# Adding the second parts of an expert's rows in PSUM with a shifted identity, and taking silu and product ahead of the transposes

## The chip, the core and the metric

The kernel runs on one core of a Trainium2 chip. What counts is device time in microseconds (us), as the median of several runs. The engines carry the names that the profile gives them: PE does matrix multiplies and PEld loads their stationary operands, DVE is the vector engine, ACT the scalar engine, POOL the general one, and SP issues most of the transfers from device memory (HBM). PE writes to PSUM only, and ACT and DVE read from there. Each engine takes its own instructions in the order in which they were written.

## What is computed

Two decoder layers on 256 positions of width 1024. Each has a mixer (gMLP and gated linear attention) and a feed-forward part; the second layer's is a mixture of eight experts, of which each position uses two. The change touches this mixture alone:

```
def swiglu(x, w_gate, w_up, w_down):
    return (jax.nn.silu(x @ w_gate) * (x @ w_up)) @ w_down

    top_val, top_idx = lax.top_k(logits, TOP_K)
    top_w = jax.nn.softmax(top_val, axis=-1)
    ...
    for e in range(N_EXPERTS):
        out = out + gates[:, e:e + 1] * swiglu(t, e_gate[e], e_up[e], e_down[e])
```

An expert's hidden width is 3584, so its three weight matrices hold 44 MB in float32, and all eight have to be read.

## The kernel before

**Precision in two parts.** Weights and activations are float32. Each is split into a high part `h`, which ACT writes as a rounded copy (`split`, L271), and a remainder `l`, which DVE gets by subtraction (L272). A product of two such numbers takes the passes high x high, high x low and low x high on PE.

**Rows of an expert.** The kernel counts at run time how many positions chose an expert, and `cases` (L964) picks one of two branches by it. With more than 64 positions ("many", a wide expert) the 128 rows of the stationary operand are 128 positions. With 64 or fewer ("few") rows 0 to 63 hold the high parts of the positions and rows 64 to 127 their remainders. One pass against the weights' high part then gives high x high in the upper half of the result and low x high in the lower half, and the pass that a wide expert needs for its remainders (`rest` in `last_passes`, L1028) falls away. The price is that the two halves have to be added later.

**Groups.** An expert's 3584 hidden columns are taken in four groups, of 512, 1024, 1024 and 1024 columns (the last expert in the opposite order). A group of 1024 fills two PSUM banks of 512 columns, so an expert has seven banks. For each group the kernel issues the gate product (`product`, tiles `eg`), the copy out of PSUM (`gated`), the up product (tiles `eu`), and `finish`. Then comes the down product of the group before (`down`, L1123 on), since the results of this one are not ready yet.

**Where the halves are added before.** In the few branch, `gated` copies the whole gate bank to `sg` in SBUF (L1075, on ACT), and `finish` copies the up bank to `up` (L1085, ACT). `finish` is a task that runs beside the next products: it lets 13 ticks pass (a tick is one step of the product loops, usually two matmuls), then does the first bank's `transposed`, and 4 ticks later the second's. The transposes are multiplies with `fold`, a 128 x 64 matrix of two identities on top of each other. Such a multiply transposes 128 columns and adds the two halves at once. Both `sg` and `up` go through it:

```
for i, t in enumerate((sg, up)):
    for j in range(4):
        nc.tensor.matmul(tp[:, j, i * HALF:i * HALF + HALF], hidden_columns(t, j), fold,
                         start=True, stop=True)
nc.scalar.activation(hid, tp[:, :, 0:HALF], AF.Silu)
nc.vector.tensor_tensor(hid, tp[:, :, HALF:P], hid, op=ALU.mult)
nc.vector.tensor_copy(ch[:, :, 0:HALF], hid)
nc.vector.tensor_tensor(ch[:, :, HALF:P], hid, ch[:, :, 0:HALF].bitcast(F32), op=ALU.subtract)
```

So silu (L1110, ACT), the product with the up half (L1111, DVE) and the two parts of the result (L1112 and L1113, DVE) come after the transposes, on 64 x 128 columns per 128 rows. The result `ch` is the stationary operand of this group's down product. A wide expert takes silu in `gated`, the product in `finish` (`times`, L714), and ordinary transposes (L1117).

**What sets the order of the weights.** SP loads the weights in units of 1 MB into 18 slots, in a fixed sequence, as soon as the program finds a slot empty (`Stream`, L169). A unit is converted, which is one L271 on ACT and one L272 on DVE into two further slots, up to 12 ticks ahead of its use; the first unit of most gate products is used unconverted instead (L1050). `tick` runs the waiting tasks and then issues the conversions that are due. The conversions thus stand on ACT and DVE between the instructions of `gated`, `finish` and `transposed`, in one sequence.

Of the kernel before, what the change touches and what calls it, by code (L numbers as in the profile page):

```python
# [39 lines left out]
def trunk(ctx: ExitStack, tc: tile.TileContext, x, w_in, gm_ws, gm_bs, gm_ln_g, gm_ln_b, gla_wa2, gla_ba,  # L40
# [17 lines left out]
    def s2(name, dt=F32, shape=(P, 512)):  # L58
        return act.tile(list(shape), dt, tag="s2", name=name, bufs=6)
# [748 lines left out]
    def moe_constants():  # L808
        iota = const.tile([P, P], F32, name="iota")
        nc.gpsimd.iota(iota, pattern=[[1, P]], base=0, channel_multiplier=0, allow_small_or_imprecise_dtypes=True)  # L810
        pri = const.tile([P, NE], F32, name="pri")
        nc.gpsimd.iota(pri, pattern=[[-1, NE]], base=NE, channel_multiplier=0, allow_small_or_imprecise_dtypes=True)
        one = const.tile([P, 1], F32, name="one")
        nc.gpsimd.memset(one, 1.0)
        ecst = const.tile([P, 2], F32, name="ecst")
        nc.gpsimd.memset(ecst, 2.718281828459045)
        pair = const.tile([2 * NE, NE], F32, name="pair")
        nc.vector.tensor_tensor(pair, ident[0:2 * NE, 0:NE], ident[0:2 * NE, NE:2 * NE], op=ALU.add)
        powers = const.tile([P, NE], F32, name="powers")
        for e in range(NE):  # L820
            nc.gpsimd.memset(powers[:, e:e + 1], float(2 ** e))

        fold = const.tile([P, HALF], F32, name="fold")
        nc.vector.tensor_tensor(fold, ident[:, 0:HALF], ident[:, HALF:P], op=ALU.add)
        return iota, pri, one.to_broadcast([P, P]), ecst, pair, fold, powers

    def moe(xT, ready, consts):
# [123 lines left out]
        class Expert:  # L951
# [36 lines left out]
            def parts(self, h, l, src):  # L988

                def few():  # L990
                    nc.scalar.activation(h[:, :, 0:HALF], src[:, :, 0:HALF], AF.Copy)
                    nc.vector.tensor_tensor(h[:, :, HALF:P], src[:, :, 0:HALF], h[:, :, 0:HALF].bitcast(F32),
                                            op=ALU.subtract)
                self.cases(few, lambda: split(h, l, src))

            def pick(self, p, src, columns=block_columns):

# [27 lines left out]
                            nc.scalar.activation(self.xw, p, AF.Copy)  # L1025
                        yield 2

            def last_passes(self, rest, last):  # L1028

                def run(ms):  # L1030
# [4 lines left out]
            def product(self, units, n, nm):  # L1035

                xh, xl = self.x
                nb = n // 512
                p = [psw(f"{nm}{b}") for b in range(nb)]
                kk = 2048 // n  # L1040
                held, rest, last = [], [], []
                for u, ((wh, wl), free, drop) in enumerate(units):
                    held.append(free)
                    for j in range(kk):
                        k = kk * u + j
                        for b in range(nb):
                            s = slice(b * 512, b * 512 + 512)
                            tick()
                            if wl is None:
                                nc.tensor.matmul(p[b], self.xw[:, k, :], wh[:, j, s], start=k == 0, stop=False,  # L1050
                                                 skip_group_check=True)
                                continue
                            nc.tensor.matmul(p[b], xh[:, k, :], wh[:, j, s], start=k == 0, stop=False,  # L1053
                                             skip_group_check=True)
                            rest.append((p[b], xl[:, k, :], wh[:, j, s], False))
                            second = p[b], xh[:, k, :], wl[:, j, s], k == KT - 1
                            if k == KT - 1 or (u % 2, j, b) == (1, kk - 1, nb - 1):
                                last.append(second)
                            else:
                                nc.tensor.matmul(*second[0:3], start=False, stop=False, skip_group_check=True)  # L1060
                    if u % 2 == 0:
                        drop()
                    if u % 2 and (nb > 1 or u == 1):
                        self.last_passes(rest, last)
                        for free in held:
                            free()
                        held, rest, last = [], [], []
                return p

            def gated(self, pg, nm):  # L1070
                t = [s2(f"sg{nm}{b}") for b in range(len(pg))]

                def all(f):
                    for o, i in zip(t, pg):
                        nc.scalar.activation(o, i, f)  # L1075
                self.cases(lambda: all(AF.Copy), lambda: all(AF.Silu))
                return t

            def finish(self, g, sg, pu, lag=13):
                nm = f"e{self.nm}{g}"  # L1080
                up = [s2(f"up{nm}{b}") for b in range(len(pu))]

                def copies():
                    for o, i in zip(up, pu):
                        nc.scalar.activation(o, i, AF.Copy)  # L1085

                def products():
                    for o, i in zip(sg, pu):
                        times(o, i)
                self.cases(copies, products)  # L1090
                self.hT[g] = []
                for b in range(len(pu)):
                    yield 4 if b else lag
                    self.hT[g].append(self.transposed(f"{nm}{b}", sg[b], up[b]))
                W.cap = len(W.plan)

            def transposed(self, nm, sg, up):
# [4 lines left out]
                hid = room[-1].tile([P, 4, HALF], F32, tag="hid", name=f"hid{nm}", bufs=2)  # L1102

                def few():

                    for i, t in enumerate((sg, up)):
                        for j in range(4):
                            nc.tensor.matmul(tp[:, j, i * HALF:i * HALF + HALF], hidden_columns(t, j), fold,  # L1108
                                             start=True, stop=True)
                    nc.scalar.activation(hid, tp[:, :, 0:HALF], AF.Silu)  # L1110
                    nc.vector.tensor_tensor(hid, tp[:, :, HALF:P], hid, op=ALU.mult)  # L1111
                    nc.vector.tensor_copy(ch[:, :, 0:HALF], hid)  # L1112
                    nc.vector.tensor_tensor(ch[:, :, HALF:P], hid, ch[:, :, 0:HALF].bitcast(F32), op=ALU.subtract)  # L1113

                def many():
                    for j in range(4):
                        nc.tensor.transpose(tp[:, j, :], hidden_columns(sg, j), ident)  # L1117
                    split(ch, cl, tp)
                self.cases(few, many)
                return ch, cl  # L1120

            def down(self, g, units, first, final):
# [92 lines left out]
        for e, ex in enumerate(experts):  # L1215
            for g, (c0, n) in enumerate(groups(e)):
# [6 lines left out]
                sg = ex.gated(ex.product(stream(gate_units(e, g)), n, f"eg{e}{g}"), f"e{e}{g}")  # L1223
# [5 lines left out]
                pu = ex.product(stream(up_units(e, g)), n, f"eu{e}{g}")  # L1229
                task = Task(ex.finish(g, sg, pu, 3 if last else 13))  # L1230
# [18 lines left out]
        with tc.If(most > P):  # L1249
# [4 lines left out]
            with tc.For_i(0, NE) as ei:  # L1254
# [27 lines left out]
                ex = Expert("z", lambda tb: rg[:, tb:tb + 1], lambda tb: rg[:, 2 + tb:3 + tb])  # L1282
                Task(ex.gather_from_scratch()).finish()
                for g in range(FE // 512):
                    sg = ex.gated(ex.product(cols_of(exp_g, g), 512, f"egz{g}"), f"ez{g}")
# [115 lines left out]
```

## Time and profile before

| | |
|---|---|
| median of 3 runs | 1342.88 us (1342.32 to 1343.03) |
| the profiled execution | 1342.48 us, of which the span is 1340.8 us |
| PE busy in the span | 97% |
| PEld busy | 76% |
| DVE busy | 80% |
| ACT busy | 63% |
| weights read | 424 MB in all |

The profile page gives the busy time of each engine, the chain of work that ended last, and groups of instructions by line with their mean duration and the idle time ahead of them. Other views show the waits by who released them, the instructions in order of time, and busy time by stretch. A matmul's end is modelled, so that one begins before the record of the last is over; what a matmul costs when many follow each other is the distance between their starts. The mixture of experts runs from about 450 us to the end.

### The profile page before, as it was taken

How to read it: one execution, taken by the hardware profiler on the slowest of the kernel's cores; microseconds unless marked ns; L12 is line 12 of the kernel's file. 1: busy time of each engine (PE TensorE's matmuls, PEld its weight loads, DVE VectorE, ACT ScalarE, POOL GpSimd, SP SyncE). 2: the span in 40 equal slices, each digit the busy share in tenths (PEclk: the TensorE clock that was granted, in tenths of full speed). 3: DMA queues.
4: the chain of work that ended last, by engine and by line, in shares of the span. 5: the costliest groups of instructions: out<-in, count | busy, mean ns of one | idle time of the engine just before them, and what ended most of it. 6: DMA issues, size and time to landing. Idle time of an engine off the chain costs nothing. (4 is left out here: it accounts for less than half of the span.)

```text
span 1340.8 us, 16964 instructions
## 1 busy us (share of the span) xinstructions
PE 1296.5 (97%) x6113; PEld 1024.0 (76%) x6113; DVE 1068.5 (80%) x965; ACT 839.0 (63%) x702; POOL 37.7 (3%) x79
## 2 busy tenths in 40 slices
PE   8999999999998999999999999999999999999996
PEld 7878888888887788777778877776776776777774
DVE  6687544476684887898888789899899989989997
ACT  5653444346342666687756667776777777877783
POOL 1012000000110000000000000000000000000000
PEclk9999999999999999999999999999999999999998
DMA  9636656543484598999999899999999999999993
GB/s 343 256 126 205 240 188 204 203 157 132 159 301 162 222 365 321 392 370 380 408 368 369 320 384 370 389 408 412 408 389 408 409 393 410 407 400 403 412 407 118
DMA packets 118766, 426.35 MB, mean 318 GB/s; under 512 B 8089, under 2 KB 10722, under 8 KB 104578
## 3 DMA queue, kind: packets, MB, share of 16 engines
q1 hardware_dynamic: 117218, 420.61, 81.0%
q0 software_dynamic: 1440, 4.33, 1.1%
q8 instruction: 64, 1.05, 0.3%
q14 instruction: 44, 0.36, 0.1%
HBM read 423.86 MB, written 1.05 MB: 317 GB/s over the span
## 5 line engine op out<-in xcount | busy, mean ns | idle before, releaser
L272 DVE TENSOR_TENSOR l<-r,h 128x2048 fp32r<-128x2048 f32 (+2 forms) x373 | 833.3, 2249 | 134.0 <-ACT h L271 117.6
L271 ACT ACTIVATE h<-r 128x2048 fp32r<-128x2048 f32 (+2 forms) x373 | 685.0, 1881 | 124.1 <-PE bank L1032 39.1
L1137 PE MATMUL bank<-h,che 128*128 128x512 f32 x440 | 174.4, 396 | 0.0
L1053 PE MATMUL eu<-h,exh 128*128 128x512 f32 x440 | 167.5, 389 | 0.0
L1144 PE MATMUL bank<-l,che 128*128 128x512 f32 x377 | 153.3, 407 | 7.0 <-DVEq L969 3.5
L1060 PE MATMUL eu<-l,exh 128*128 128x512 f32 x361 | 141.0, 391 | 0.3 <-DVE l L272 0.3
L1053 PE MATMUL eg<-h,exh 128*128 128x512 f32 x316 | 128.2, 418 | 0.0
L1050 PE MATMUL eg<-r,xw 128*128 128x512 f32 x248 | 114.5, 595 | 0.0
L1144 PEld LDWEIGHTS bank<-l,che 128*128 128x128 f32 x377 | 70.8, 188 | 41.9 <-DVE l L272 17.1
L1053 PEld LDWEIGHTS eu<-h,exh 128*128 128x128 f32 x440 | 82.6, 188 | 16.9
L1137 PEld LDWEIGHTS bank<-h,che 128*128 128x128 f32 x440 | 82.8, 188 | 15.2
L1060 PE MATMUL eg<-l,exh 128*128 128x512 f32 x237 | 92.7, 391 | 0.1
L1060 PEld LDWEIGHTS eu<-l,exh 128*128 128x128 f32 x361 | 67.8, 188 | 15.9 <-DVE l L272 2.1
L1050 PEld LDWEIGHTS eg<-r,xw 128*128 128x128 f32 x248 | 45.2, 190 | 39.6 <-issue 37.8
L266 PE MATMUL f<-h,xhm 128*128 128x512 f32 (+1 forms) x192 | 72.2, 376 | 0.0
L267 PE MATMUL f<-l,xhm 128*128 128x512 f32 (+1 forms) x192 | 71.4, 372 | 0.0
L268 PE MATMUL f<-h,xlm 128*128 128x512 f32 (+1 forms) x192 | 71.4, 372 | 0.0
L1053 PEld LDWEIGHTS eg<-h,exh 128*128 128x128 f32 x316 | 59.5, 188 | 15.4 <-issue 4.1
L1110 ACT ACTIVATE hide<-bank 128x256 f32<-128x256 f32 x42 | 16.1, 384 | 71.7 <-PE bank L1108 71.7
L1060 PEld LDWEIGHTS eg<-l,exh 128*128 128x128 f32 x237 | 44.6, 188 | 12.7 <-issue 3.8
L1075 ACT ACTIVATE sge<-eg 128x512 f32<-128x512 f32 x55 | 30.2, 595 | 36.4 <-PE eg L1032 36.3
L1108 PEld LDWEIGHTS bank<-fold,sge 128*128 128x128 f32 x336 | 46.0, 196 | 5.2 <-issue 2.4
(354 smaller groups left out, 1803.3 us busy)
## 6 DMA issues: line engine op xcount, KB each, us to landing
r<-in_exp_w_gate SPq DMA_DIRECT2D x112, 1024.0 KB, 11.1
r<-in_exp_w_up SPq DMA_DIRECT2D x112, 1024.0 KB, 7.5
r<-in_exp_w_down SPq DMA_DIRECT2D x110, 1024.0 KB, 11.6
r<-in_w_in SPq DMA_DIRECT2D x17, 1024.0 KB, 8.5
r<-in_ffn_w_gate SPq DMA_DIRECT2D x11, 1024.0 KB, 6.9
r<-in_ffn_w_up SPq DMA_DIRECT2D x11, 1024.0 KB, 5.3
r<-in_ffn_w_down SPq DMA_DIRECT2D x11, 1024.0 KB, 4.9
r<-in_w_out SPq DMA_DIRECT2D x8, 1024.0 KB, 9.2
```

The costliest lines, as they stand in the source:

```text
L266: nc.tensor.matmul(ps, xh, wh, start=start, stop=False)
L267: nc.tensor.matmul(ps, xh, wl, start=False, stop=False)
L268: nc.tensor.matmul(ps, xl, wh, start=False, stop=stop)
L271: nc.scalar.activation(dst_h, src, AF.Copy)
L272: nc.vector.tensor_tensor(dst_l, src, dst_h.bitcast(F32), op=ALU.subtract)
L1050: nc.tensor.matmul(p[b], self.xw[:, k, :], wh[:, j, s], start=k == 0, stop=False, skip_group_check=True)
L1053: nc.tensor.matmul(p[b], xh[:, k, :], wh[:, j, s], start=k == 0, stop=False, skip_group_check=True)
L1060: nc.tensor.matmul(*second[0:3], start=False, stop=False, skip_group_check=True)
L1075: nc.scalar.activation(o, i, f)
L1108: nc.tensor.matmul(tp[:, j, i * HALF:i * HALF + HALF], hidden_columns(t, j), fold, start=True, stop=True)
L1137: nc.tensor.matmul(y, ch[:, k, :], wh[:, j, s], start=first and u + j == 0, stop=False, skip_group_check=True)
L1144: nc.tensor.matmul(y, ch[:, k, :], wl[:, j, s], start=False, stop=False, skip_group_check=True)
```

## The change

In the few branch the lower half of each gate bank and each up bank is now copied to SBUF alone (`second_parts`: 64 rows by 512 columns, on ACT). A matmul with `fold[64:128]`, an identity that takes rows 64 to 127 to rows 0 to 63, adds it onto the upper half that still stands in PSUM (`folded`). For the gate bank this is put behind the passes of the second unit of the up product, inside `last_passes`, and silu follows there on 64 rows. For the up bank it is put 6 ticks into the next down product, followed by the product with silu on DVE, in a branch of its own. The transposes come 7 ticks later and 4 ticks after that, so at the same ticks as before (3 and 4 for the last group, which had 3). They are true transposes of 64 rows now, of one tensor, and the two parts of the result are taken straight from PSUM by `parts`. The tiles `up` and `hid` go; `second` (two buffers) comes. Wide experts compute what they did.

```
-        fold = const.tile([P, HALF], F32, name="fold")
+        fold = const.tile([P, HALF], F32R, name="fold")
...
-            def last_passes(self, rest, last):
+            def last_passes(self, rest, last, few=None):
...
-                self.cases(lambda: run(last), lambda: run([*rest, *last]))
+                    if then:
+                        then()
+                self.cases(lambda: run(last, few), lambda: run([*rest, *last], None))
+
+            def folded(self, p, t):
+
+                nc.tensor.matmul(p[0:HALF], fold[HALF:P, :], t[HALF:P, :], start=False, stop=True,
+                                 skip_group_check=True)
...
-                        self.last_passes(rest, last)
+                        self.last_passes(rest, last, few if u == 1 else None)
...
+            def second_parts(self, ps, nm):
+
+                t = [room[-1].tile([P, 512], F32R, tag="second", name=f"{nm}{b}", bufs=2) for b in range(len(ps))]
+
+                def copies():
+                    for o, i in zip(t, ps):
+                        nc.scalar.activation(o[HALF:P], i[HALF:P], AF.Copy)
+                return t, copies
+
             def gated(self, pg, nm):
...
+                bg, copies = self.second_parts(pg, f"bg{nm}")
+                sg = [s2(f"sg{nm}{b}") for b in range(len(pg))]
...
+                self.cases(copies, many)
+
+                def later():
+                    for i, t in zip(pg, bg):
+                        self.folded(i, t)
+                    for o, i in zip(sg, pg):
+                        nc.scalar.activation(o[0:HALF], i[0:HALF], AF.Silu)
+                return sg, later
+
+            def finish(self, g, sg, pu, lag=(6, 7)):
...
+                bu, copies = self.second_parts(pu, f"bu{nm}")
...
                 self.cases(copies, products)
+                yield lag[0]
+
+                def few():
+                    for i, t in zip(pu, bu):
+                        self.folded(i, t)
+                    for o, i in zip(sg, pu):
+                        nc.vector.tensor_tensor(o[0:HALF], i[0:HALF], o[0:HALF], op=ALU.mult)
+                if self.wide is not None:
+                    self.cases(few, lambda: None)
...
                 def few():
...
+                    for j in range(4):
+                        nc.tensor.transpose(tp[:, j, 0:HALF], hidden_columns(sg[0:HALF], j), ident[0:HALF, 0:HALF])
```

How this moves instructions is shown for one group of 1024 columns. Both branches of a case stand in such a list, the many branch first; `L969` rows are the branches themselves.

ACT in the up product, where the conversions `h` of four units stand. Before:

```order
L271 ACTIVATE h_6278<-r_6037 128x2048
L271 ACTIVATE h_6288<-r_6049 128x2048
L969 COMPARE_AND_BRANCH
L969 UNCONDITIONAL_BRANCH x2
L271 ACTIVATE h_6316<-r_6053 128x2048
L271 ACTIVATE h_6326<-r_6073 128x2048
```

and with the change:

```order
L271 ACTIVATE h_6254<-r_6020 128x2048
L271 ACTIVATE h_6264<-r_6032 128x2048
L969 COMPARE_AND_BRANCH
L969 UNCONDITIONAL_BRANCH
L1109 ACTIVATE sge_6243<-eg_6123 64x512
L1109 ACTIVATE sge_6244<-eg_6124 64x512
L969 UNCONDITIONAL_BRANCH
L271 ACTIVATE h_6296<-r_6036 128x2048
L271 ACTIVATE h_6306<-r_6061 128x2048
```

The two silus of the group have come between the second and the third conversion.

PE at the first bank's transposes, in the down product of the group before. Before:

```order
L1117 MATMUL bank_3525<-ident,sge_6267 128x128 x4
L969 UNCONDITIONAL_BRANCH
L1108 MATMUL bank_3525<-fold,sge_6267 128x64 x4
L1108 MATMUL bank_3525<-fold,upe_6353 128x64 x4
L969 UNCONDITIONAL_BRANCH
```

and with the change, here and some ticks ahead (the two rows of L1047):

```order
L1047 MATMUL eu_6250<-bue_6333,fold 64x512
L1047 MATMUL eu_6251<-bue_6334,fold 64x512
L969 UNCONDITIONAL_BRANCH
...
L969 COMPARE_AND_BRANCH
L1147 MATMUL bank_3525<-ident,sge_6243 128x128 x4
L969 UNCONDITIONAL_BRANCH
L1143 MATMUL bank_3525<-ident,sge_6243 128x64 x4
L969 UNCONDITIONAL_BRANCH
```

Eight multiplies with `fold` per bank have become four transposes, and one addition per bank stands ahead of them.

DVE in the same stretch. Before:

```order
L272 TENSOR_TENSOR l_6363<-r_6113,h_6362 128x2048
L969 COMPARE_AND_BRANCH
L969 UNCONDITIONAL_BRANCH x2
L272 TENSOR_TENSOR l_6399<-r_6228,h_6398 128x2048
L272 TENSOR_TENSOR l_6409<-r_6246,h_6408 128x2048
L969 COMPARE_AND_BRANCH
L272 TENSOR_TENSOR cle_6415<-bank_3525,che_6414 128x512
L969 UNCONDITIONAL_BRANCH
L1111 TENSOR_TENSOR hide_6416<-bank_3525,hide_6416 128x256
L1112 CAST che_6414<-hide_6416 128x4x64
L1113 TENSOR_TENSOR che_6414<-hide_6416,che_6414 128x4x64
```

and with the change:

```order
L272 TENSOR_TENSOR l_6343<-r_6094,h_6342 128x2048
L969 COMPARE_AND_BRANCH
L969 UNCONDITIONAL_BRANCH
L1126 TENSOR_TENSOR sge_6243<-eu_6250,sge_6243 64x512
L1126 TENSOR_TENSOR sge_6244<-eu_6251,sge_6244 64x512
...
L272 TENSOR_TENSOR l_6384<-r_6202,h_6383 128x2048
L272 TENSOR_TENSOR l_6394<-r_6220,h_6393 128x2048
...
L994 TENSOR_TENSOR che_6399<-bank_3525,che_6399 128x4x64
```

The group's two products now stand two conversions ahead of the transposes' results, and one subtraction per bank is left behind them. The sequence of SP's transfers is what it was.

## Rows read from the trace of the kernel before

**Rows 1.** The page: busy time, share of the span, instructions.

```profile
PE 1296.5 (97%) x6113; PEld 1024.0 (76%) x6113; DVE 1068.5 (80%) x965; ACT 839.0 (63%) x702; POOL 37.7 (3%) x79
```

**Rows 2.** Busy us by stretch: PE PEld DVE ACT POOL, PE clock, DMA share, GB/s.

```profile
676.40:795.50 119.10, 119.10 (x541) 95.93 (x540) 94.82 (x61) 74.46 (x55) 0.00 (x0) 1.00 0.91 354
1021.50:1130.70 109.20, 105.23 (x492) 80.69 (x491) 99.61 (x74) 81.77 (x65) 0.00 (x0) 1.00 1.02 404
820.00:1310.00 490.00, 473.74 (x2210) 363.08 (x2209) 450.28 (x329) 369.20 (x293) 0.00 (x0) 1.00 1.01 405
1150.00:1160.00 10.00, 10.00 (x58) 8.42 (x57) 8.56 (x10) 5.16 (x5) 0.00 (x0) 1.00 1.02 422
```

**Rows 3.** Waits, 560 to 1341 us: us in total, times, longest.

```profile
ACT hide L1110 <- PE bank L1108: 71.1, 38, 3.4
...
DVE l L272 <- DVEq L969: 4.1, 15, 0.3
...
SPq L169 <- DVE l L272: 404.7, 91, 11.1
```

**Rows 4.** DVE's waits in one few expert, 1021.5 to 1130.7 us.

```profile
DVE l L272 <- ACT h L271: 5.8, 7, 2.5
```

**Rows 5.** Groups by line and form, 500 to 1341 us: count, busy us, mean ns.

```profile
L1108 PE MATMUL bank<-fold,sge 128*128 128x64 f32 x336 | 43.8, 273 | 0.0
...
L1075 ACT ACTIVATE sge<-eg 128x512 f32<-128x512 f32 x51 | 28.0, 595 | 35.4 <-PE eg L1032 35.3
...
L1085 ACT ACTIVATE upe<-eu 128x512 f32<-128x512 f32 x42 | 23.0, 599 | 6.8 <-PE eu L1032 6.8
...
L1113 DVE TENSOR_TENSOR che<-hide,che 128x256 fp32r<-128x256 f32 x42 | 17.9, 426 | 1.4
...
L1111 DVE TENSOR_TENSOR hide<-bank,hide 128x256 f32<-128x256 f32 x42 | 17.6, 419 | 3.1 <-ACT hide L1110 3.1
...
L1110 ACT ACTIVATE hide<-bank 128x256 f32<-128x256 f32 x42 | 16.1, 384 | 71.7 <-PE bank L1108 71.7
...
L1112 DVE CAST che<-hide 128x256 fp32r<-128x256 f32 x42 | 12.3, 294 | 1.4
...
L714 DVE TENSOR_TENSOR sge<-eu,sge 128x512 f32<-128x512 f32 x9 | 5.8, 683 | 1.1 <-PE eu L1032 1.1
```

**Rows 6.** PE in order of time in a few expert: start us, us, instruction. Two stretches.

```profile
1041.97 1.04 PE L1108 MATMUL bank<-fold,sge 128*128 128x64 f32 x8
1042.85 1.11 PE L1108 MATMUL bank<-fold,upe 128*128 128x64 f32 x8
...
1058.60 0.39 PE L1137 MATMUL bank<-h,che 128*128 128x512 f32 x1
...
1060.06 0.40 PE L1137 MATMUL bank<-h,che 128*128 128x512 f32 x1
1060.29 0.39 PE L1144 MATMUL bank<-l,che 128*128 128x512 f32 x1
```

**Rows 7.** PE in order of time in a wide expert.

```profile
769.78 0.63 PE L1117 MATMUL bank<-ident,sge 128*128 128x128 f32 x4
770.17 0.48 PE L1137 MATMUL bank<-h,che 128*128 128x512 f32 x1
```

**Rows 8.** ACT in order of time from a group's second fold on.

```profile
1047.72 0.38 ACT L1110 ACTIVATE hide<-bank 128x256 f32<-128x256 f32 x1 [3.35 <-PE bank L1108]
1048.01 3.71 ACT L271 ACTIVATE h<-r 128x2048 fp32r<-128x2048 f32 x2
...
1052.56 7.33 ACT L271 ACTIVATE h<-r 128x2048 fp32r<-128x2048 f32 x4
1059.78 1.09 ACT L1085 ACTIVATE upe<-eu 128x512 f32<-128x512 f32 x2
```

**Rows 9.** DVE in order of time, same stretch.

```profile
1048.14 0.42 DVE L1111 TENSOR_TENSOR hide<-bank,hide 128x256 f32<-128x256 f32 x1 [0.65 <-ACT hide L1110]
...
1049.94 13.84 DVE L272 TENSOR_TENSOR l<-r,h 128x2048 fp32r<-128x2048 f32 x6 [0.59 <-ACT h L271]
```

More of the change, by code (lines that the diff above doesn't have):

```diff
@@ L993, in few, with many @@
                                             op=ALU.subtract)
-                self.cases(few, lambda: split(h, l, src))
+                def many():
+                    if first_many:
+                        first_many()
+                    split(h, l, src)
+                self.cases(few, many)
             def pick(self, p, src, columns=block_columns):
@@ L1026, in gather, with run, product @@
                         yield 2
-            def last_passes(self, rest, last):
-                def run(ms):
+            def last_passes(self, rest, last, few=None):
+                def run(ms, then):
                     for ps, x, w, stop in ms:
                         nc.tensor.matmul(ps, x, w, start=False, stop=stop, skip_group_check=True)
-                self.cases(lambda: run(last), lambda: run([*rest, *last]))
-            def product(self, units, n, nm):
+                    if then:
[4 more added lines that the diff above has]
+                                 skip_group_check=True)
+            def product(self, units, n, nm, few=None):
                 xh, xl = self.x
@@ L1068, in product, with many @@
                 return p
-            def gated(self, pg, nm):
[L1071 to L1079, printed above, removed]
+            def second_parts(self, ps, nm):
[4 more added lines that the diff above has]
+                return t, copies
+            def gated(self, pg, nm):
+                bg, copies = self.second_parts(pg, f"bg{nm}")
+                sg = [s2(f"sg{nm}{b}") for b in range(len(pg))]
+                def many():
+                    for o, i in zip(sg, pg):
+                        nc.scalar.activation(o, i, AF.Silu)
+                self.cases(copies, many)
+                def later():
+                    for i, t in zip(pg, bg):
+                        self.folded(i, t)
+                    for o, i in zip(sg, pg):
+                        nc.scalar.activation(o[0:HALF], i[0:HALF], AF.Silu)
+                return sg, later
+            def finish(self, g, sg, pu, lag=(6, 7)):
                 nm = f"e{self.nm}{g}"
[L1081 to L1085, printed above, removed]
+                bu, copies = self.second_parts(pu, f"bu{nm}")
                 def products():
@@ L1101, in transposed @@
                 cl = act.tile([P, 4, P], F32R, tag="cl", name=f"cl{nm}", bufs=4)
-                hid = room[-1].tile([P, 4, HALF], F32, tag="hid", name=f"hid{nm}", bufs=2)
                 def few():
[L1106 to L1113, printed above, removed]
+                    for j in range(4):
+                        nc.tensor.transpose(tp[:, j, 0:HALF], hidden_columns(sg[0:HALF], j), ident[0:HALF, 0:HALF])
                 def many():
@@ L1117, in many @@
                         nc.tensor.transpose(tp[:, j, :], hidden_columns(sg, j), ident)
-                    split(ch, cl, tp)
-                self.cases(few, many)
+                self.parts(ch, cl, tp, few, many)
                 return ch, cl
@@ L1222, in moe @@
                     most = nc.values_load(cnt_i[0:1, 0:1], min_val=0, max_val=2 * P)
-                sg = ex.gated(ex.product(stream(gate_units(e, g)), n, f"eg{e}{g}"), f"e{e}{g}")
+                sg, later = ex.gated(ex.product(stream(gate_units(e, g)), n, f"eg{e}{g}"), f"e{e}{g}")
                 if (e, g) == (0, 1):
@@ L1228, in moe @@
                     W.cap = W.index[up_units(e, g)[-1]] + 2
-                pu = ex.product(stream(up_units(e, g)), n, f"eu{e}{g}")
-                task = Task(ex.finish(g, sg, pu, 3 if last else 13))
+                pu = ex.product(stream(up_units(e, g)), n, f"eu{e}{g}", later)
+                task = Task(ex.finish(g, sg, pu, (3, 4) if last else (6, 7)))
                 W.cap = len(W.plan) - 2 if last else len(W.plan)
@@ L1284, in moe @@
                 for g in range(FE // 512):
-                    sg = ex.gated(ex.product(cols_of(exp_g, g), 512, f"egz{g}"), f"ez{g}")
+                    sg, _ = ex.gated(ex.product(cols_of(exp_g, g), 512, f"egz{g}"), f"ez{g}")
                     pu = ex.product(cols_of(exp_u, g), 512, f"euz{g}")
```

10 lines of the change are left out of this document (6 added, 4 removed).

## The prediction

> **What bounds the kernel.** I read the busy line of the page first [rows 1]. PE stands at 97% of the span and DVE at 80%, which would make PE the bound and every microsecond taken off it worth a microsecond. But matmuls overlap in their records, and the mixture has two kinds of expert, so I read the busy times by stretch next [rows 2]. In a wide expert PE is busy for all 119.1 us and the transfers run at 354 GB/s: there PE is the limit. The change alters nothing that such an expert computes. A few expert takes 109.2 us, and there is no single limit in it. PE has 105.2 busy, DVE 99.6, and the transfers fill their engines (a share of 1.02) at 404 GB/s. Three resources stand within a tenth of their limit, so a saving on one can be worth no more than the others leave.
>
> Who waits for whom comes from the waits [rows 3]. SP waits 404.7 us in total for DVE's `l`: a weight is loaded when DVE has set its slot free, so the transfers follow DVE, and nowhere are they the last to arrive. DVE is idle for 109.2 - 99.6 = 9.6 us of a few expert, and 5.8 of these, in seven waits, end with an `h` from ACT [rows 4]. ACT in turn waits for PE: 71.1 us in 38 waits before the silu behind the fold multiplies [rows 3], against 35.3 before L1075 and 6.8 before L1085 [rows 5]. The chain is therefore fold multiplies on PE, then ACT blocked in its sequence by silu, then a late `h`, then DVE idle, then a slot that is set free late. In one place it can be followed by the clock. ACT sat 3.35 us before silu of a second bank at 1047.72 and began the next conversion only at 1048.01 [rows 8]; DVE idled 0.65 us before its product and 0.59 before the next `l` at 1049.94 [rows 9].
>
> **PE, removed and added.** Per bank of a few expert go the eight multiplies with `fold`. The four of the gate start at 1041.97 and the four of the up half at 1042.85, 0.88 us apart [rows 6]; twice that is 1.76 us. What comes is two additions of 512 columns and four transposes. No row shows such an addition. The nearest is a pass over the same 512 columns, with 0.23 us from one start to the next (1060.06 to 1060.29) [rows 6]. I take 0.23, with 0.11 below (half the rows, half the time) and 0.51 above (0.23 plus one fold record of 0.273 [rows 5] uncovered). Four transposes of 128 columns stood in 0.39 us of a wide expert (769.78 to 770.17) [rows 7], and I take that; the new ones have half the rows and could cost 0.20, or 0.22 each as a fold multiply does (1.76 / 8), so 0.88. Together 2 x 0.23 + 0.39 = 0.85, so 0.91 a bank is saved, and 38 us over the 42 banks. The bounds are 0.42 and 1.90 a bank: 56 us saved to 6 us lost. That is PE's own account, not the kernel's.
>
> Beside this row stands a rule. The Trainium skill, TensorE: Matmul & The Clock Gate, Part 4: PE-mode transpose, gives about 275 ns for one 128 x 128 transpose in a kernel. The trace does not agree as far as cost in a row goes: four together took 0.39 us [rows 7]. By the page's figure the bank would cost 0.46 + 1.10, the saving would be 0.20 a bank (an estimate), and the kernel's time about 1340.
>
> **ACT.** Per bank go two copies of 0.595 and 0.599 and a silu of 0.384 [rows 5], 1.58 us. What comes is two copies of the lower halves, a silu on 64 x 512 and a rounded copy of 64 x 512 out of PSUM, in the shape of the old silu. The first three keep 512 columns. No row has 64 rows, so I take the full 0.595 (half of it is the lower bound), and 0.384 for the last: 2.17 us. That is 0.59 more a bank and 25 us over all, or 4.2 in each few expert. It is hidden as long as ACT has idle time there: 109.2 - 81.8 = 27.4 us [rows 2]. The lower bound would make it 12 us less in all.
>
> **DVE.** Per bank go 0.419, 0.294 and 0.426 [rows 5]. What comes is a product on 64 x 512, taken as the 0.683 of L714 (half as the lower bound), and one subtraction of 0.426. That is 1.11 against 1.14, so 1 us in all, which I leave out. The work moves, though: the products stand two conversions ahead, and behind the transposes only the subtraction is left, so DVE's chain at that place is shorter by 0.29 + 0.42 us a bank.
>
> **Branches.** Each group gains one more branch on PE, DVE and ACT, in wide experts an empty one. DVE's waits on a branch came 15 times and cost 4.1 us, 0.27 each [rows 3]. For four new ones an expert I take half, 0.5 us, between 0 and 1.1. In the two wide experts that makes 1 us. SP's sequence of transfers stays, POOL has no part in it.
>
> **The sum.** Of ACT's waits for PE the fold multiplies hold 71.1 of 71.1 + 35.3 + 6.8, or 63%. I put the same share of DVE's 5.8 us down to them: 3.6 us a few expert. ACT waits 71.1 / 6 = 11.9 us at this place in an expert, and the new work of 4.2 us takes about a third of what an earlier release gives, which leaves 3.6 x 0.65 = 2.4. Less 0.5 for branches it is 1.9 us. Six few experts give 11.4, and the wide ones take 1: 10.4 us. The bounds are a loss of 1 per few expert, where nothing of the wait goes, and a gain of 9.6, where DVE never waits again. The profiled execution took 1342.48 us, 0.4 below the median of 1342.88; 1342.9 - 10.4 gives **1332.5 us**. What is late next is DVE itself, then the transfers. Over 820 to 1310 us they moved 405 GB/s, and in the best 10 us that I found 422 [rows 2]. At that rate 490 us would be 19.7 shorter and six few experts 26 shorter, which bounds the gain at 1323 and 1317.
>
> **Rivals.**
> - *The gain stays with PE.* DVE's work is as long as before, and DVE sets the pace through the slots. For it: 99.6 of 109.2 us busy, and only 3.1 us in the whole stage in which DVE's product waited for silu [rows 5]. Against it: the 5.8 us that it waits for ACT [rows 4]. Then only branches and small shifts remain: about 1341. The Trainium skill, Perfetto Trace Analysis, Identifying the Most-Contended Engine, leans to this side: it tells a reader to judge DVE by occupancy, but not TensorE by matmul busy time, since pipelined instructions mislead. The rows agree, in that a few expert has PE 105 busy and still waits on DVE.
> - *The up copies come too late (slower).* ACT runs four conversions without a break from 1052.56 and gets to the two copies of the up bank at 1059.78, ready at 1060.87 [rows 8]. The down product began at 1058.60, and at 0.46 us a tick the new additions are due five or six ticks later, at 1060.9 to 1061.4 [rows 6]. Before, nothing asked for them so early. Two silus now stand among those conversions and push the copies back by 1.19 us, to 1062.1. PE and, behind it, DVE's product would then wait some 1.2 us a group, with further `l` queued behind on DVE. Over 24 groups that is 29 us, over half of them 14. Without the gain the time is 1357 to 1371, with it 1347 to 1361; I write 1350. Against it: DVE was then in an unbroken run of 13.84 us from 1049.94 [rows 9] and reaches the product only after the addition, so PE pays from what it has saved. It decides where the addition ends later than DVE's previous `l`.
> - *PE is the bound after all.* Then its 38 us count in full, less branches: about 1305. Against it: the transfers, which would have to exceed 422 GB/s by far.
> - *PE saves only half.* With transposes at the price of a fold multiply, 0.88 a bank, the saving is 0.42 in place of 0.91, and the gain shrinks with it, to 1338.
>
> **How the numbers follow.** The forecast has a chance of 0.62, with 1319 to 1340 of its own. The gain staying with PE has 0.15, late up copies 0.12, PE as the bound 0.05, half the saving 0.06. The range runs from 1319, between the two caps by the transfers, to 1343, which takes in the first and last rival; it leaves out the slower one and PE as the bound. A measurement of this kernel tells about 0.2% from no change, 2.7 us. Faster than 1340.2 are the forecast, PE as the bound and half the saving: 0.73. Same is the gain staying with PE: 0.15. Slower are late up copies: 0.12.
>
> **What the profile after would show.** If I am right, the additions follow the passes around them at 0.23 us and the four transposes take 0.2 to 0.4 us. ACT's waits for the fold, 71.1 us before, fall below half; ACT is busy 15 to 25 us more in all. DVE's busy time stays within 3 us, its idle time in a few expert falls from 9.6 to about 7.5, and a few expert takes about 107 us at some 411 GB/s. Wide experts keep 119 us. A few expert of 109 us with DVE's waits for `h` unchanged would show the first rival. Idle time of PE before the additions, put down to ACT's copies, together with longer idle time of DVE, would show the second. Rates over 422 GB/s would show that the cap by the transfers was not one.

## The result and the profile after

The change made the kernel slower: 1374.05 us (1373.86 to 1374.74) against 1342.95, a ratio of 1.0233 with a 95% interval of 1.0215 to 1.0251. The forecast was 1332.5, in a range of 1319 to 1343.

The busy line of the profile page comes first. PE is busy for the same 1297 us in a span that is 32 us longer [rows 1], although 7% of its instructions are gone (6113 before). DVE has 3 us less to do, ACT 31 more.

```profile
PE 1296.9 (94%) x5693; PEld 985.2 (72%) x5693; DVE 1065.3 (78%) x923; ACT 869.6 (63%) x744; POOL 37.5 (3%) x79
```

Busy time by stretch, columns as in [rows 2]. The first row is the few expert that took 109.2 us before, from the same point of its first gate product to that of the next. It takes 114.7, at 391 GB/s in place of 404, and the granted clock is 0.96. The second row is 2.8 us out of it in which PE worked 0.65. The third is the 3.41 us that soon follow, with the clock at 0.50: 1.2 in place of 2.4 GHz.

```profile
1035.50:1150.20 114.70, 107.09 (x421) 75.44 (x420) 98.89 (x67) 86.74 (x72) 0.00 (x0) 0.96 0.99 391
...
1074.50:1077.30 2.80, 0.65 (x2) 0.20 (x2) 2.52 (x2) 2.72 (x3) 0.00 (x0) 1.00 1.03 413
...
1078.05:1081.46 3.41, 3.41 (x9) 2.65 (x10) 2.82 (x3) 0.71 (x1) 0.00 (x0) 0.50 1.05 416
```

The waits of the stage: us in total, times, longest. ACT's wait in the transposed part, 71.1 us before [rows 3], falls below half, as forecast. What is new is PE's waits ahead of the up bank's addition (L1047). ACT's waits for PE to set the slots of `h` free have grown from 26.4 to 63.1 us, and DVE's for ACT from 56.0 to 86.9. In that one few expert DVE waits 12.7 us for `h`; it was 5.8 [rows 4]. Before:

```profile
DVE l L272 <- ACT h L271: 56.0, 53, 3.6
...
ACT h L271 <- PE bank L1032: 26.4, 20, 4.2
```

and with the change:

```profile
DVE l L272 <- ACT h L271: 86.9, 71, 6.0
ACT h L271 <- PE bank L1040: 63.1, 21, 5.0
ACT che L993 <- PE bank L1143: 33.9, 24, 4.2
...
PE eu L1047 <- ACT h L271: 24.5, 12, 2.2
...
PE eu L1047 <- DVEq L969: 6.5, 5, 2.4
...
PE bank L1143 <- DVE sge L1126: 6.2, 6, 4.6
```

What each instruction costs, in the groups by line and form, against [rows 5]. ACT's four come to 2.15 us a bank and DVE's two to 1.09.

```profile
L1126 DVE TENSOR_TENSOR sge<-eu,sge 64x512 f32<-64x512 f32 x42 | 27.0, 674 | 0.0
...
L1092 ACT ACTIVATE bge<-eg 64x512 fp32r<-64x512 f32 x42 | 23.0, 589 | 23.6 <-PE eg L1040 23.4
L1092 ACT ACTIVATE bue<-eu 64x512 fp32r<-64x512 f32 x42 | 23.0, 588 | 2.6 <-PE eu L1040 2.1
L1109 ACT ACTIVATE sge<-eg 64x512 f32<-64x512 f32 x42 | 22.9, 587 | 4.0 <-PE eg L1047 3.4
...
L994 DVE TENSOR_TENSOR che<-bank,che 128x256 fp32r<-128x256 f32 x42 | 16.6, 417 | 1.3 <-ACT che L993 1.3
L993 ACT ACTIVATE che<-bank 128x256 fp32r<-128x256 f32 x42 | 16.2, 385 | 34.4 <-PE bank L1143 33.9
```

**PE at one addition.** PE in order of time, with its idle time in brackets: the last pass ahead of the addition starts at 1074.79, the addition at 1077.32. Behind it a pass takes 0.43 us from start to start, before it 0.23.

```profile
1074.79 0.50 PE L1173 MATMUL bank<-l,che 128*128 128x512 f32 x1
1077.32 0.65 PE L1047 MATMUL eu<-bue,fold 64*64 64x512 f32 x2 [2.03 <-ACT h L271]
1077.89 0.68 PE L1166 MATMUL bank<-h,che 128*128 128x512 f32 x1
1078.38 0.63 PE L1173 MATMUL bank<-l,che 128*128 128x512 f32 x1
1078.80 0.63 PE L1166 MATMUL bank<-h,che 128*128 128x512 f32 x1
```

The view names ACT's `h` as the releaser. ACT in order of time says that the copies which the addition reads were done 2.0 us before, at 1075.31 (1074.23 + 1.08), and that the `h` behind them ended at 1077.24:

```profile
1074.23 1.08 ACT L1092 ACTIVATE bue<-eu 64x512 fp32r<-64x512 f32 x2
1075.33 1.91 ACT L271 ACTIVATE h<-r 128x2048 fp32r<-128x2048 f32 x1
```

The addition does not read that `h`. On DVE, though, an unbroken run of conversions ended at 1077.12, 0.2 us before the addition:

```profile
1070.12 7.00 DVE L272 TENSOR_TENSOR l<-r,h 128x2048 fp32r<-128x2048 f32 x3
1077.39 2.29 DVE L272 TENSOR_TENSOR l<-r,h 128x2048 fp32r<-128x2048 f32 x1 [0.27 <-ACT h L271]
```

ACT and DVE end together here. In another group they don't. There ACT's `h` ended at 1225.69, DVE's `l` at 1225.94, and the addition came at 1226.14, the same 0.20 us behind DVE. PE, then ACT, then DVE:

```profile
1223.24 0.51 PE L1173 MATMUL bank<-l,che 128*128 128x512 f32 x1
1226.14 0.64 PE L1047 MATMUL eu<-bue,fold 64*64 64x512 f32 x2 [2.40 <-DVEq L969]
```

```profile
1223.78 1.91 ACT L271 ACTIVATE h<-r 128x2048 fp32r<-128x2048 f32 x1
```

```profile
1223.65 2.29 DVE L272 TENSOR_TENSOR l<-r,h 128x2048 fp32r<-128x2048 f32 x1 [0.47 <-ACT bue L1092]
1226.21 2.29 DVE L272 TENSOR_TENSOR l<-r,h 128x2048 fp32r<-128x2048 f32 x1 [0.27 <-DVEq L969]
```

The trace has DVE's signal as well: of the instructions that `cases` (L969) puts on DVE's queue between 1074 and 1078 us, one is a semaphore event, at 1077.2, behind the run of conversions and ahead of the addition.

```profile
L969 DVEq EVENT_SEMAPHORE  x1: 21/21/21, 1077.2 to 1077.2; - x1
```

It is the same at all 18 additions that come over 1 us late: 17 start 0.20 us behind the end of a conversion on DVE and one 0.33, while ACT's copies had been done for 1.9 to 2.4 us. In five of them, each 1.2 us late, ACT ran nothing between the copies and the addition.

So PE waits for DVE to get past a branch. The program says why: `finish` begins with a branch in whose many side DVE's product (`times`) reads the up banks. In a few expert nothing is done there, but the addition overwrites these banks, so it is ordered behind that branch on DVE. DVE comes to it only behind the conversions that stand ahead of it. That is the **first theory**: the loss is this wait, and the lower clock behind it. The **second theory** is that ACT's four new instructions per group delay its conversions.

### The profile page after: what moved, and what is told of

Read it like the earlier page. It is cut to its first block, busy times and chain, and to the rows that moved or that the text cites. A ratio compares the mean times of both kernels' runs of the same rounds, so it can differ in the third digit from the quotient of the medians.

```text
span 1372.5 us, 16423 instructions
## 1 busy us (share of the span) xinstructions
PE 1296.9 (94%) x5693; PEld 985.2 (72%) x5693; DVE 1065.3 (78%) x923; ACT 869.6 (63%) x744; POOL 37.5 (3%) x79
## 5 line engine op out<-in xcount | busy, mean ns | idle before, releaser
L1166 PE MATMUL bank<-h,che 128*128 128x512 f32 x440 | 186.5, 424 | 2.8 <-PEq L969 2.8
L1166 PEld LDWEIGHTS bank<-h,che 128*128 128x128 f32 x440 | 87.4, 199 | 34.4 <-issue 15.8
L1173 PEld LDWEIGHTS bank<-l,che 128*128 128x128 f32 x377 | 74.6, 198 | 20.0 <-DVE l L272 5.1
L1076 PEld LDWEIGHTS eg<-l,exh 128*128 128x128 f32 x237 | 44.6, 188 | 12.7 <-issue 4.1
L1047 PE MATMUL eu<-bue,fold 64*64 64x512 f32 x42 | 15.5, 440 | 32.2 <-ACT h L271 24.5
L271 ACT ACTIVATE chf<-thf 128x512 fp32r<-128x512 f32 (+1 forms) x12 | 6.7, 561 | 61.2 <-PE thf L382 61.2
L268 PEld LDWEIGHTS f<-h,xlm 128*128 128x128 f32 x192 | 36.2, 188 | 6.4
```

The costliest lines, as they stand in the source:

```text
L268: nc.tensor.matmul(ps, xl, wh, start=False, stop=stop)
L1047: nc.tensor.matmul(p[0:HALF], fold[HALF:P, :], t[HALF:P, :], start=False, stop=True, skip_group_check=True)
L1166: nc.tensor.matmul(y, ch[:, k, :], wh[:, j, s], start=first and u + j == 0, stop=False, skip_group_check=True)
L1173: nc.tensor.matmul(y, ch[:, k, :], wl[:, j, s], start=False, stop=False, skip_group_check=True)
```

## The experiments

In the tables, "few expert" is a third of the time from ACT's first `yh` (the high part of an expert's result) of one expert to that of the third after it, over the same three few experts. "Gaps" are the start-to-start distances ahead of a group's first up addition beyond a pass's 0.23 us, summed over the groups where such a distance is over 0.45; the expectations have 35.2 for the 36.7 us of the change. The row of the kernel before has the medians of its runs beside the others.

**Taking the wait away.** own_branch:

```
-                self.cases(copies, products)
+                if self.wide is not None:
+                    self.cases(copies, lambda: None)
                 yield lag[0]
...
-                if self.wide is not None:
-                    self.cases(few, lambda: None)
+                self.cases(few, products)
```

> Edit: DVE's product of a wide expert moves from the branch before the addition into the branch of the addition, so that no instruction of DVE that reads the up banks stands ahead of PE's addition, and DVE has no branch at that place. First theory (PE waits at the addition for DVE to reach an empty branch that stands behind its conversions, and PE's clock falls after such a wait): the 35.2 us of gaps ahead of the up additions fall below 12, PE keeps full clock in the stage, and the time is 1320 to 1343 us. Second theory (ACT's four new instructions per group make its conversions late): the gaps may shrink but the time stays within 1362 to 1376 us.

**Moving the addition.** adds_late changes `(6, 7)` to `(10, 7)`, adds_early to `(3, 10)`.

> Edit: the additions of the up bank stand 10 ticks into the down product in place of 6, the transposes still 7 ticks behind them. First theory: 4 ticks are 1.84 us, so of a 2.07 us wait 0.2 to 0.5 us is left; gaps ahead of the up additions below 10 us in all, the time 1325 to 1345 us. Second theory: ACT's sequence is what it was up to the transposes, so the time is 1365 to 1380 us.

> Edit: the additions of the up bank stand 3 ticks into the down product in place of 6, the transposes 10 ticks behind them and so where they were. First theory: each wait grows by 3 ticks or 1.38 us, also where there was none, over 23 groups up to 32 us more: 1385 to 1410 us, with more stretches at half clock. Second theory: nothing on ACT changes, 1370 to 1378 us.

**The wait alone, in the kernel before.** before_plus_wait:

```
...
                 self.cases(copies, products)
+                yield min(6, lag - 3)
+                def few():
+                    for i in pu:
+                        nc.tensor.matmul(i[0:HALF], foldr[HALF:P, :], spare[HALF:P, :], start=True, stop=True,
+                                         skip_group_check=True)
+                if self.wide is not None:
+                    self.cases(few, lambda: None)
...
```

> Edit to the kernel before: a branch 6 ticks into the down product in which PE writes 64 x 512 sums that nothing reads over each up bank of a few expert, with the folding as it was. PE pays 42 such matmuls (12 us of its own time at 0.29 each) and waits for the same things as the additions of the change. First theory: it waits for DVE's branch as the change does, some 35 us of gaps, and the kernel gets 20 to 45 us slower than before, 1363 to 1388 us. Second theory: without the new work on ACT the kernel is within 12 us of before, 1343 to 1355 us.

Then before_plus_adds takes DVE out of it, with the edit of own_branch, and before_plus_branch has an empty branch in its place.

> Edit to before_plus_wait: DVE's product of a wide expert moves into the branch of the added matmuls, as in own_branch, so that PE waits there for ACT's copies alone. It has the same 42 matmuls and the same branch. If the wait for DVE is the price in before_plus_wait (1403.5 us), this run is 1345 to 1366 us: at most PE's own 12 us for the matmuls and some 10 for branches above 1342.7. If the matmuls and the branch themselves cost the 61 us, it is 1390 to 1404 us.

> Edit to the kernel before: an empty branch 6 ticks into each down product, and nothing else. It prices the added branch alone. In own_branch a group of a wide expert is 0.75 us longer than before, at the step from the down product to the next gate product. If the branch is the cause, the wide experts lose 5 to 7 us together and the kernel 6 to 18, so 1348 to 1360 us. If the branch is hidden and it was the product's new place that cost the 0.75 us, the time is 1342 to 1345 us.

| run | time, us | ratio to before (95%) | few expert, us | gaps, us |
|---|---|---|---|---|
| before | 1342.7 to 1343.6 | | 109.1 | |
| the change | 1374.05 | 1.0233 (1.0215 to 1.0251) | 113.0 | 36.7 |
| own_branch | 1344.87 | 1.0013 (1.0003 to 1.0023) | 107.5 | 0.3 |
| adds_late | 1352.91 | 1.0074 (1.0058 to 1.0091) | 108.3 | 1.8 |
| adds_early | 1424.12 | 1.0605 (1.0587 to 1.0623) | 120.6 | 69.0 |
| before_plus_wait | 1403.53 | 1.0455 (1.0436 to 1.0475) | 118.6 | 39.2 |
| before_plus_adds | 1361.90 | 1.0142 (1.0125 to 1.0159) | 111.0 | 0.8 |
| before_plus_branch | 1342.73 | 1.0001 (0.9992 to 1.0011) | 109.0 | |

The first theory holds, from both sides. Taking DVE's product out from ahead of the addition gives 29.2 us back (1374.05 to 1344.87), with ACT's work as it was; the time is 2 us above the range that was given, for which the runs further down account. The clock was not full throughout: there is one stretch of 3.4 us at 1.2 GHz in the stage and one of 6.8 in the last group, beside the kernel's last microseconds, where the kernel before has one too. In the groups of own_branch the addition no longer shows a wait worth the name:

```profile
L1047 PE MATMUL eu<-bue,fold 64*64 64x512 f32 x42 | 14.8, 420 | 0.2 <-ACT bue L1092 0.2
```

Three ticks earlier the gaps nearly double and 50 us are lost, more than the 11 to 36 that were expected. In the kernel before, the wait by itself (with the lower clock behind it) is worth 1403.53 - 1361.90 = 41.6 us. before_plus_wait is 15 us above the top of its range, since the matmuls and their branch cost 19 us more without the wait (before_plus_adds), which lies within what was expected of that run. The wait's row among PE's waits there puts it down to DVE's queue at the branch (line 975 in that kernel):

```profile
PE eu L1101 <- DVEq L975: 32.4, 17, 2.2
```

adds_late takes the gaps away as expected, but lands 8 us above its range. Its transposes moved too, to 17 and 21 ticks, and runs further down show that such a move can cost time; that it does so here was not tried.

The empty branch costs nothing. The time is that of the second reading, but its cause does not hold either: it is not the branch as such, and not the product's new place, since the change as made has the same loss in wide experts with the product where it was. A branch of its own with matmuls in it makes a group of a wide expert 0.7 to 0.8 us longer although they are jumped over: between the gate products that start at 700.9 and 774.4 us of the kernel before lie two groups of a wide expert, 73.5 us. With the change they take 75.1 and in before_plus_adds 75.0. So my cost of a branch, taken from DVE's waits, missed PE's.

**What own_branch still loses.** Few experts are 1.6 us faster there than before, six times, and yet the whole is 2 us slower. One part are the wide experts. Another is the end: from the start of the last two down products, which follow each other, to the last instruction the kernel before took 29.2 us, the change 34.2 and own_branch 35.2. PE, then DVE, in order of time in own_branch's last group:

```profile
1310.77 0.44 PE L1047 MATMUL eu<-bue,fold 64*64 64x512 f32 x1 [0.15 <-ACT bue L1092]
1317.92 0.71 PE L1143 MATMUL bank<-ident,sge 64*128 64x64 f32 x4 [4.68 <-DVE sge L1127]
```

```profile
1312.69 4.49 DVE L272 TENSOR_TENSOR l<-r,h 128x2048 fp32r<-128x2048 f32 x2 [2.94 <-ACT h L271]
1317.10 0.68 DVE L1127 TENSOR_TENSOR sge<-eu,sge 64x512 f32<-64x512 f32 x1
```

The product's operands are there soon after 1310.77, DVE is idle until 1312.69, but two conversions stand ahead of the product. The transposes, and PE for 4.68 us, wait for it. Before the change PE took the copies straight into its fold multiplies, and DVE came behind. The same wait is there in the other groups, 22 times and 19.2 us in all:

```profile
PE bank L1143 <- DVE sge L1127: 19.2, 22, 4.7
```

own_branch_tail puts the last addition and product at once behind the copies: `(3, 4) if last` becomes `(0, 5) if last`, and a lag of 0 does not yield.

> Edit to own_branch: in the last group of the last expert the addition and DVE's product come at once behind the copies and not 3 ticks later, where two conversions have got ahead of the product on DVE. In own_branch the time from the last down product but one to the end is 6.0 us longer than before, with PE waiting 4.68 us for that product and at half clock for 6.8 us behind it. If the product's place behind the conversions is the cause, this run is 1338 to 1341 us and that stretch at most 31 us; if the last weights set the end, it stays at 1344 to 1346 us.

inside_passes, tail_transposes_15, tail_transposes_15_17 and inside_15_17 move the transposes, and the two "inside" runs also the additions, by this among other lines:

```
...
-                            self.last_passes(rest[hf] if ending else rest[0] + rest[1], last)
+                            then, self.then = (self.then, (None, None)) if (u, n) == (1, 3) else ((None, None),) * 2
+                            self.last_passes(rest[hf] if ending else rest[0] + rest[1], last, *then)
...
```

> Edit to own_branch_tail: where the down product belongs to the same expert, the up bank's additions and the product run inside the branch of its last passes (8 ticks in), so that the separate branch goes; and the transposes come at 16 ticks in place of 13, behind DVE's product. First reading (what own_branch still loses are the branch, 6 us, and PE's 15 us of waits for the product ahead of the transposes): 1322 to 1336 us, gaps ahead of the transposes below 5 us. Second reading (DVE and the transfers are the ceiling, so no wait of PE matters any more): 1337 to 1342 us.

> Edit to own_branch_tail: the transposes of the first bank come 15 ticks into the down product in place of 13, the second bank's 4 ticks later as before. In own_branch_tail PE waits 0.5 to 1.1 us for DVE's product ahead of 22 first transposes, 15.5 us in all; 2 ticks are 0.92 us. If PE is what the few experts wait for, this run is 1324 to 1335 us. If DVE and the transfers are the ceiling, it is 1337 to 1340 us. If later transposes run into the gathering of the next expert's rows, as the waits for L994 and L1008 in inside_passes suggest, it is above 1340 us.

> Edit to own_branch_tail: first bank's transposes at 15 ticks, the second bank's 2 ticks later, so at 17 as before. As the run before, but with the second bank at its old place: if only the wait for the product mattered, both give the same; if the collision with the gathering did, this one is 3 us or more below it. Expected 1324 to 1335 us if PE is what the few experts wait for, 1337 to 1340 us if it is DVE and the transfers.

> Edit to inside_passes: transposes at 15 and 17 ticks in place of 16 and 20. It undoes the later place of the second bank and keeps the additions in the branch of the last passes. If the place of the transposes made inside_passes 15.7 us slower than own_branch_tail, this run is below 1342 us, and with the 0.7 us a group of the wide experts saved below tail_transposes_15_17 by 2 to 6 us. If having the additions inside the last passes was the cause, it stays at 1350 to 1356 us.

| run | transposes at ticks | time, us | ratio to before (95%) | few expert, us |
|---|---|---|---|---|
| own_branch_tail | 13, 17 | 1338.70 | 0.9972 (0.9961 to 0.9983) | 107.5 |
| inside_passes | 16, 20 | 1354.42 | 1.0095 (1.0078 to 1.0112) | 110.4 |
| tail_transposes_15 | 15, 19 | 1359.76 | 1.0117 (1.0100 to 1.0133) | 110.3 |
| tail_transposes_15_17 | 15, 17 | 1338.23 | 0.9964 (0.9950 to 0.9978) | 106.5 |
| inside_15_17 | 15, 17 | 1332.92 | 0.9927 (0.9910 to 0.9944) | 106.5 |

own_branch_tail gains 6.2 us over own_branch, and its end takes 27.3 us. Two ticks for the first bank alone bring a few expert from 107.5 to 106.5, but hardly show in the whole (the intervals overlap). The time is in the range of the reading in which DVE and the transfers are the ceiling; the few expert's gain of 1.0 us is not what that reading says. The trace shows where most of it goes: the three experts gain 3.0 us, and the one behind them takes 118.4 us in place of 115.8, with ACT waiting 3.6 us for weights that have not landed. own_branch_tail has no such wait there, so at this place the weights are the last to arrive. ACT in order of time:

```profile
1229.77 1.91 ACT L271 ACTIVATE h<-r 128x2048 fp32r<-128x2048 f32 x1 [2.27 <-DMA r<-in_exp_w_gate]
1232.98 1.91 ACT L271 ACTIVATE h<-r 128x2048 fp32r<-128x2048 f32 x1 [1.30 <-DMA r<-in_exp_w_gate]
```

Two ticks for the second bank as well cost 21.5 us; the granted clock is 0.982 there and 0.993 in tail_transposes_15_17. In that run the waits of the stage show ACT and DVE in the gathering of the next expert's rows (`exh`), in rows that are far smaller in tail_transposes_15_17 and own_branch (8.1 and 1.7 us):

```profile
ACT exh L993 <- PE bank L1007: 26.9, 7, 5.6
...
DVE exh L994 <- ACT exh L993: 19.1, 5, 4.3
```

The second bank's transposes at 19 ticks fall into the next gate product, where the gathering stands. That the second bank's place decides is shown by the pair. That the gathering is the mechanism was argued and not tried, and lateness alone does not bring it about: adds_late has the second bank at 21 ticks, with 9.6 and 1.7 us in these rows.

So inside_passes, above both of its readings, had its transposes in the wrong place: with them at 15 and 17 the same additions inside the last passes make the fastest kernel, 5.3 us below tail_transposes_15_17, as was expected. In inside_15_17 the wide expert's two groups are back at 73.5 us, and 820 to 1310 us have 408 GB/s, near the 405 of before [rows 2].

```profile
820.00:1310.00 490.00, 473.45 (x1914) 329.37 (x1914) 452.56 (x300) 399.96 (x332) 0.00 (x0) 0.99 1.02 408
```

It beats the kernel before by 0.7% and the change by 41 us.

## Why the prediction was wrong

**The step that failed** is the term for the new branch, which had no wait of PE in it. Under "Branches" I took from the trace what a branch costs DVE, 0.27 us when it waits at one, put 0.5 us on a few expert, and asked only what stands in the new branch. I did not ask which engine's earlier instructions the addition is ordered behind. It writes a bank that an instruction of DVE reads in the *other* side of an earlier branch, and DVE gets to that branch late. PE waited 1.2 to 2.7 us for it in 18 of 24 groups, 36 us in all, and taking the wait away gave 29 us back. The 1 us for the two wide experts was too small as well: at 0.75 us a group their eight groups make 6 us (an estimate).

**The rival that ended on the slower side** had the symptom, PE idle ahead of the additions, but the wrong releaser, ACT's copies, and half the size: 1.2 us a group, where most waits were 2.3, and 1347 to 1361 us, or 1371 without the gain, where 1374 was measured. The copies were ready 2.0 us before the addition in the group shown, and in own_branch, where the addition waits for them alone, 0.3 us is left. Its point of decision pointed at the wrong place too: I held DVE's unbroken run of conversions against it, as cover. That run was the cause.

**PE's saving** was put at 0.91 us a bank. PE in order of time, in the changed kernel: two additions together take 0.59 us (1068.05 to 1068.64) and four transposes 0.61 (1085.55 to 1086.16).

```profile
1068.05 0.66 PE L1047 MATMUL eg<-bge,fold 64*64 64x512 f32 x2
1068.64 0.50 PE L1069 MATMUL eu<-h,exh 128*128 128x512 f32 x1
...
1085.55 0.69 PE L1143 MATMUL bank<-ident,sge 64*128 64x64 f32 x4
1086.16 2.84 PE L1066 MATMUL eg<-r,xw 128*128 128x512 f32 x6
```

The eight old multiplies stood in 16 records, two for each, 0.11 us from start to start [rows 6]; each of the new matmuls is one record. A bank thus costs 0.59 + 0.61 = 1.20 and not 0.85, and 0.56 of 1.76 is saved, 24 us and not 38. Both terms lie within their bounds. The transposes were taken from a wide expert's, at 0.39 for four; the half-sized ones take longer, 0.15 each. The Trainium skill, TensorE: Matmul & The Clock Gate, Part 4: PE-mode transpose, gives about 275 ns for one of 128 x 128; neither size comes near that in a row here. Its direction was right: the new transposes cost more than I took.

**What a microsecond of PE is worth.** I held DVE and the transfers to set the pace of a few expert and gave PE's saving a small share. before_plus_adds speaks against that: 7 banks x 0.295 us = 2.1 us more of PE made a few expert of the kernel before 1.9 us longer. PE's time counted there almost in full, if the branch that holds the matmuls costs a few expert nothing, which no run separates. The Trainium skill, Perfetto Trace Analysis, Identifying the Most-Contended Engine, which judges DVE by occupancy and discounts matmul busy time, leant the other way, and the measurement decides. In the other direction it does not count in full: own_branch and inside_15_17 save 7 x 0.56 = 3.9 us of PE in a few expert and gain 1.6 and 2.6. My 1.9 us a few expert was near that by luck: these runs do not confirm the reckoning from DVE's waits that gave it.

**ACT and DVE** came as forecast: 2.15 us a bank against 2.17, and 1.09 against 1.11. ACT's wait in the transposed part fell below half, too. What ACT's 31 us more of work cost, no run tells apart; own_branch bounds it, since there few experts are faster than before with all of it in place.

**The clock** was in no term. The mean granted clock fell from 0.996 of 1340.8 us to 0.982 of 1372.5, so some 19 us of full-speed PE time went with it (24.7 - 5.4), an estimate. In own_branch it is 0.990. Of 13 additions that waited 2.3 us or more beyond a pass, 6 came with a stretch at 1.2 GHz, which began in the wait or soon behind it. What the wait would have cost without the clock is left open: no run separates the two.

**The end of the kernel** was not in the sum at all. The product that moved ahead of the transposes makes the last transposes depend on the product's place in DVE's sequence, 5 to 6 us on a path that nothing covers (34.2 and 35.2 against 29.2 us), and own_branch_tail gets 6.2 back.

## What to carry to other kernels

When a change adds a write to a buffer, look at every instruction ahead of it in program order that touches this buffer, in branches that are not taken too, and ask how late its engine gets there; the order of one engine's rows does not show this, the sequence of the engine that it waits for does. Where two engines end together, look for a group in which they don't before you believe the releaser that a view names. Moving a step of a busy engine ahead of another engine's step turns the first one's backlog into a wait, and in the last group of a kernel into time.

## What the runs showed of the hardware

- Four transposes of 64 x 128 took 0.61 us where four of 128 x 128 took 0.39 [rows 7].
- A branch of its own that jumps over two matmuls made a group of a wide expert 0.7 to 0.8 us longer on PE; an empty one, nothing; and with the same two matmuls in a branch that was there before, two groups took 73.5 us, as before.
- Half the rows did not make an instruction shorter: a copy of 512 columns took 0.589 us on ACT for 64 rows and 0.595 for 128, and a product on DVE 0.674 and 0.683 [rows 5].
- After some waits of 2.3 us PE ran at 1.2 GHz, with 0.43 us a pass in place of 0.23; after others of the same length it kept 2.4 GHz.
